# The account that sets the order of instructions: a margin on each TensorE matmul, and a lower DMA rate

## The chip, the cores and the metric

The kernel runs on one NeuronCore of one Trainium2 chip. A core has TensorE (PE, matmuls into PSUM), VectorE (DVE), ScalarE (ACT), GpSimd (POOL) and SyncE (SP, which here issues nearly all DMAs), each with an instruction queue of its own that runs in order. The metric is the device time of one launch in microseconds; several runs are given by their median. Profiles are read by engine and by line of the kernel.

## The reference

It is one inference step of a two-layer trunk over 640 tokens (128 context, 512 latent), width 2048, in fp32:

```python
for l in range(DEPTH):                        # DEPTH = 2, once for context, once for latent tokens
    shift, scale, gate = modulation(c, ada_w[l], ada_b[l])        # silu(c) @ w + b, split in 3
    h = rms_norm(x, norm_g[l]) * (1 + scale) + shift
    if l % 2 == 0:   # [A] windowed attention, 8 heads, sink logit, 2-D rotary  || [B] gated linear attention, 4 heads
        y, _ = even_mixer(h, w_in_even[e], ...)
    else:            # [C] 2-D neighbourhood attention, 8 heads, learned bias    || [D] spatial-gating MLP, 8 column tiles
        y, _ = odd_mixer(h, w_in_odd[o], ...)
    x = x + gate * ((y * silu(gate columns)) @ w_out[l])
y = rms_norm(x, final_norm_g)
```

The projections (`h @ w_in`, `y @ w_out`) make up most of the matmul work. The outputs are the normed tokens, and keys, values and scan states of the context.

## The kernel before

Activations are kept transposed, features on the 128 partitions, tokens along the free axis. A "chunk" is 128 output columns of a weight matrix. Each fp32 product is made of three matmuls on a rounded high part and a low rest: `acth*whi`, `actl*whi`, `acth*wlo`, in halves of 320 (or 322) columns. These "main matmuls" are some 11,900 of the 13,136 PE instructions. Weights come by DMA into `wraw` or `rs`, ACT rounds them into `whi` (in the first stage `suhi`), POOL or DVE subtracts to get `wlo` (`sulo`). Many chunk pairs share work by a Strassen-like scheme with sums of activations (`eh`, `el`, `tail`) and of weights.

No hardware scheduler and no fixed text decides the order. While the program is built, a class `Pace` keeps an account: a clock for each engine (`t["t"]` for PE, `v`, `a`, `g` for DVE, ACT, POOL, `q` for DMA issue, `d` for the DMA stream), and for each piece of a tile when it will be written and read. `Trunk.now` is the account's PE time. After each main matmul or two, `tick` is called: it emits DMAs whose buffer is free by the account, weight splits (`wpump`) whose engines are not too far ahead, deferred evacuations, and one or more steps of generator tasks (a softmax block, a transposition, a scan). A task that needs a result waits with `until`, which lets PE go on with main matmuls as long as the account says that the result is not there yet:

```python
def left(self, *aps):          # how long until these are ready, by the account
    return max(0.0, pc.ready("t", [], spans) - self.now)
def until(self, *aps):
    while not self.force and self.left(*aps) > 0.05:
        yield self.left(*aps)
```

So the account's prices set where the small matmuls and transpositions of the tasks stand among the main matmuls, in which order DVE, ACT, POOL and SP get their instructions, and nothing else: the real waits are semaphores.

The first stage, `start`, is of its own kind. Sixteen times (feature tile f = 0 to 15) four 512 KB pieces of modulation weights (`Y<-ada` and `more<-ada`, a ring of ten buffers) go through four narrow matmuls each (line 1603, 32 output partitions, written `bank<-Y,cond` or `bank<-more,cond`; the trace has two records for each). ACT copies the sums to `adas`, PE turns them (`bank<-ident,adas`, line 401), DVE makes scale and shift from them (`sh`, `A`), ACT and DVE make `acth` and `actl` of tile f, POOL adds the tile's squares (`ssq`). Between these stand the main matmuls of the first eight chunks. Chunks 0 and 1 ("lead", banks 67 to 70) run along with f; chunks 2 to 7 run in "windows" of 2 to 4 tiles into banks 73 and 74, and DVE adds each window to a sum in SBUF (`Y<-Y,bank`, `tail<-tail,bank`, `part_b<-part_b,bank`). A window can start when DVE has emptied its bank.

Every engine instruction but PE's is recorded at line 210, main matmuls at 396, DMA issues at 434.

Of the kernel before, what the change touches and what calls it, by code (L numbers as in the profile page):

```python
# [235 lines left out]
class Trunk:  # L236
# [166 lines left out]
    def pe(self, cost, out, *ins, narrow=False):  # L403
        pc = self.pace
        o, i = [pc.span(out)], [pc.span(x) for x in ins]
        if pc.late:
            pc.due(o + i)
        at = pc.ready("t", o, i)
        if narrow != self.narrow:
            self.narrow = narrow  # L410
            at = max(self.now, at) + 0.15
        self.now = pc.t["t"] = max(self.now, at) + cost
        pc.note("t", o, i, self.now)

    narrow = False
# [6 lines left out]
    def dma(self, out, in_):  # L422

        pc = self.pace
        o, i = [pc.span(out)], [pc.span(in_)]
        if pc.late:
            pc.due(o + i)
        n = int(np.prod(out.shape)) * 4

        def emit():  # L430
            at = pc.t["q"] = max(pc.t["q"], self.now, pc.ready("q", o, i)) + 0.45
            pc.t["d"] = max(pc.t["d"], at + 1.2) + max(0.09, n / 400e3)
            pc.note("q", o, i, pc.t["d"] + 1.0)
            self.nc.sync.dma_start(out, in_)  # L434

        if pc.ready("q", o, i) <= self.now + 0.1:
            emit()
        else:
            pc.late.append((emit, o + i, lambda: pc.ready("q", o, i)))
# [2622 lines left out]
```

## Time and profile before

| | |
|---|---|
| median of 3 runs | 2100.67 us (2098.91 to 2102.41) |
| the profiled execution's own time | 2107.35 us |
| its span, first to last instruction | 2105.6 us |
| mean granted TensorE clock in it | 0.989 of full |
| busy shares of the span: PE, DVE, POOL, ACT | 97%, 72%, 52%, 46% |
| instructions | 38934 |

The profile lists busy time by engine, the span in 40 slices, who waited for whom, and instructions in order of time. Matmuls overlap each other in the records, so the pitch from start to start tells more of PE than the length of one. The profiled execution is 6.7 us above the median of the runs.

### The profile page before, as it was taken

The page shows a single profiled execution, that of the slowest core. Times are in us where ns is not written, and L with a number is a line of the kernel's source. Part 1 is how long each engine was busy: PE and PEld are TensorE (multiplying, and loading weights), DVE is VectorE, ACT ScalarE, POOL GpSimd, SP SyncE. Part 2 cuts the span into 40 slices and gives each one's busy share as a digit, 9 for nine tenths or more (in the row PEclk, how much of TensorE's full clock was granted, in tenths as well). Part 3 has the DMA queues.
Part 4 walks back from the last instruction along what each step waited for, and adds up shares of the span by engine and source line. Part 5 has one row for each costly group of instructions (what it writes and reads, how often), then busy time and mean ns, then how long its engine had stood idle before and what let it go on. Part 6 is the DMA issues. An engine that isn't in the chain of part 4 may idle for free. (4 is left out here: it accounts for less than half of the span.)

```text
span 2105.6 us, 38934 instructions
## 1 busy us (share of the span) xinstructions
PE 2041.9 (97%) x13930; PEld 1969.8 (94%) x13930; DVE 1519.5 (72%) x3468; ACT 964.1 (46%) x2001; POOL 1091.3 (52%) x827
## 2 busy tenths in 40 slices
PE   7899999999999999999999999999999999999996
PEld 4688999999999999999989999999999999999995
DVE  2447788887878787798766878878775567676565
ACT  4334454343334545444454444445554554454443
POOL 3346333233222223566556666756566567757783
PEclk9999999999999999999999999999999999999998
DMA  9943334346544443777648867756655575567766
GB/s 375 377 156 116 124 111 132 123 128 197 167 147 140 122 141 116 245 247 224 177 145 272 269 199 226 244 195 207 229 186 185 180 259 189 197 222 224 237 198 209
DMA packets 215874, 412.52 MB, mean 196 GB/s; under 512 B 25664, under 2 KB 88320, under 8 KB 215680
## 3 DMA queue, kind: packets, MB, share of 16 engines
q1 hardware_dynamic: 214208, 408.43, 58.8%
q8 instruction: 109, 1.79, 0.3%
q10 hardware_dynamic: 1472, 1.61, 0.2%
q14 instruction: 85, 0.70, 0.1%
HBM read 368.88 MB, written 38.45 MB: 193 GB/s over the span
## 5 line engine op out<-in xcount | busy, mean ns | idle before, releaser
L396 PE MATMUL bank<-acth,whi 128*128 128x320 f32 (+1 forms) x3112 | 958.4, 319 | 21.1 <-DVE part_b L210 6.5
L396 PE MATMUL bank<-acth,wlo 128*128 128x320 f32 (+1 forms) x3112 | 932.8, 311 | 3.4 <-POOL wlo L210 3.3
L396 PE MATMUL bank<-actl,whi 128*128 128x320 f32 (+1 forms) x3112 | 931.1, 311 | 0.0
L210 POOL TENSOR_TENSOR wlo<-wraw,whi 128x512 fp32r<-128x512 f32 x359 | 501.7, 1403 | 687.1 <-ACT whi L210 633.5
L396 PEld LDWEIGHTS bank<-acth,whi 128*128 128x128 f32 x3112 | 580.9, 190 | 36.6 <-issue 12.3
L396 PEld LDWEIGHTS bank<-acth,wlo 128*128 128x128 f32 x3112 | 580.2, 189 | 6.4 <-POOL wlo L210 6.0
L396 PEld LDWEIGHTS bank<-actl,whi 128*128 128x128 f32 x3112 | 580.7, 190 | 1.8
L210 POOL TENSOR_TENSOR wlo<-rs,whi 128x512 fp32r<-128x512 f32 x293 | 407.6, 1404 | 205.6 <-ACT whi L210 172.9
L210 ACT ACTIVATE whi<-wraw 128x512 fp32r<-128x512 f32 x393 | 241.2, 624 | 178.4 <-PE bank L396 101.1
L210 ACT ACTIVATE whi<-rs 128x512 fp32r<-128x512 f32 x329 | 198.9, 624 | 82.9 <-PE bank L396 52.1
L210 DVE CUSTOM_DVE_ANT_0 adas<-adas,bank,partg 128x256 bf16<-128x256 f32 (+1 forms) x320 | 178.0, 556 | 22.3 <-ACT bank L210 11.8
L396 PE MATMUL bank<-tail,whi 128*128 128x322 f32 (+1 forms) x672 | 152.2, 314 | 0.2 <-DMA tail<-far_dram 0.2
L210 ACT ACTIVATE arena<-arena,bc 128x128 f32<-128x128 f32 (+3 forms) x167 | 83.4, 519 | 137.7 <-DVE bc L210 97.0
L396 PE MATMUL bank<-eh,whi 128*128 128x322 f32 (+1 forms) x444 | 138.9, 313 | 0.0
L396 PE MATMUL bank<-eh,wlo 128*128 128x322 f32 (+1 forms) x444 | 137.8, 310 | 0.5 <-DVE wlo L210 0.5
L396 PE MATMUL bank<-el,whi 128*128 128x322 f32 (+1 forms) x444 | 137.9, 311 | 0.0
L210 ACT ACTIVATE Y<-bank 128x128 f32<-128x128 f32 (+5 forms) x134 | 52.0, 410 | 143.3 <-PE bank L396 73.0
L210 ACT ACTIVATE sums<-bank 128x320 f32<-128x320 f32 (+1 forms) x125 | 54.4, 435 | 129.7 <-PE bank L396 122.3
L210 DVE TENSOR_TENSOR rs<-rs 128x512 f32<-128x512 f32 x83 | 92.9, 1129 | 28.5 <-POOL wlo L210 23.4
L396 PEld LDWEIGHTS bank<-tail,whi 128*128 128x128 f32 x672 | 112.2, 189 | 0.8 <-DMA tail<-far_dram 0.8
L210 DVE TENSOR_TENSOR bank<-bank,sums 128x320 f32<-128x320 f32 (+1 forms) x162 | 76.3, 492 | 50.1 <-PE bank L396 41.3
L396 PE MATMUL bank<-tail,wlo 128*128 128x322 f32 (+1 forms) x336 | 104.0, 310 | 0.4 <-POOL wlo L210 0.4
(227 smaller groups left out, 2886.6 us busy)
## 6 DMA issues: line engine op xcount, KB each, us to landing
tail<-far_dram SPq DMA_DIRECT2D x196, 322.0 KB, 4.5
wraw<-w_even SPq DMA_DIRECT2D x176, 256.0 KB, 3.3
adas<-ada_g SPq DMA_DIRECT2D x128, 256.0 KB, 3.8
adas<-ada SPq DMA_DIRECT2D x128, 256.0 KB, 3.6
rs<-w_odd SPq DMA_DIRECT2D x63, 512.0 KB, 5.4
wraw<-w_odd SPq DMA_DIRECT2D x37, 512.0 KB, 5.4
more<-ada SPq DMA_DIRECT2D x36, 512.0 KB, 8.1
rs<-w_out SPq DMA_DIRECT2D x30, 512.0 KB, 5.5
```

Of the source, the lines that this page charges most:

```text
L210: return f(*args, **kw)
L396: self.nc.tensor.matmul(out, lhsT, rhs, start=start, stop=stop, **kw)
```

## The change

Two prices of the account are changed, and nothing else:

```diff
@@ def pe(self, cost, out, *ins, narrow=False): @@
-        self.now = pc.t["t"] = max(self.now, at) + cost
+        self.now = pc.t["t"] = max(self.now, at) + cost + 0.0025
@@ def dma(self, out, in_): emit() @@
-            pc.t["d"] = max(pc.t["d"], at + 1.2) + max(0.09, n / 400e3)
+            pc.t["d"] = max(pc.t["d"], at + 1.2) + max(0.09, n / 330e3)
```

The price of a 320-column main matmul goes from 0.1473 to 0.1498 us, that of a 512 KB transfer from 1.31 to 1.59 us. PE has the same 13,136 instructions, SP the same 1388 DMAs. Three weight subtractions go from DVE (364 to 361 of that shape) to POOL (661 to 664), and ACT has 24 table loads in place of 30. The main matmuls after the first stage stand in the same order as before; what stands between them moves.

First place, PE in the first stage, at the tiles f = 4 and 5: `bank_72<-ident,adas` are the transpositions after which DVE can make the next tile's `actl`. Before:

```order
L401 MATMUL bank_72<-ident,adas 128x128 x2
L396 MATMUL bank_74<-acth,whi 128x320
L396 MATMUL bank_74<-actl,whi 128x320
L396 MATMUL bank_74<-acth,wlo 128x320
L396 MATMUL bank_74<-acth,whi 128x320
L396 MATMUL bank_74<-actl,whi 128x320
L396 MATMUL bank_74<-acth,wlo 128x320
L1603 MATMUL bank_71<-more_116,cond_112 32x256 x8
L396 MATMUL bank_73<-acth,suhi_225 128x322
```

Now:

```order
L401 MATMUL bank_72<-ident,adas 128x128 x2
L396 MATMUL bank_73<-acth,whi 128x322
L396 MATMUL bank_73<-actl,whi 128x322
L396 MATMUL bank_73<-acth,wlo 128x322
L396 MATMUL bank_73<-acth,whi 128x322
L396 MATMUL bank_73<-actl,whi 128x322
L396 MATMUL bank_73<-acth,wlo 128x322
L1603 MATMUL bank_71<-more_116,cond_112 32x256 x4
L396 MATMUL bank_74<-acth,whi 128x320
```

The transpositions stand one group of six earlier among the window matmuls (after the 108th main matmul of the program, before after the 114th), and the narrow matmuls come piece by piece (x4) where two pieces (x8) stood together. In the whole stage the 64 pieces make 47 separate groups, where they made 33, and the last piece comes after the 480th main matmul, where it came after the 384th.

Second place, DVE in the first stage, around main matmul 228 (tile f = 9 before, f = 8 now): `actl` belongs to the next tile, `tail` and `part_b` empty the window banks. Before:

```order
L210 TENSOR_TENSOR tail_81<-tail_81,bank_74 128x320
L210 SCALAR_TENSOR_TENSOR actl<-Y,A_98,acth 128x128
L210 SCALAR_TENSOR_TENSOR actl<-Y,A_98,acth 128x512
L210 TENSOR_TENSOR actl<-sh_771,acth 128x2
L210 TENSOR_TENSOR tail_81<-tail_81,bank_73 128x320
L210 TENSOR_TENSOR part_b<-part_b,bank_73 128x2
```

Now:

```order
L210 TENSOR_TENSOR part_b<-part_b,bank_73 128x2
L210 SCALAR_TENSOR_TENSOR actl<-Y,A_98,acth 128x128
L210 SCALAR_TENSOR_TENSOR actl<-Y,A_98,acth 128x512
L210 TENSOR_TENSOR actl<-sh_742,acth 128x2
L210 TENSOR_TENSOR tail_81<-tail_81,bank_74 128x320
L210 TENSOR_TENSOR tail_81<-tail_81,bank_73 128x320
L210 TENSOR_TENSOR part_b<-part_b,bank_73 128x2
```

The three `actl` instructions stand one bank earlier: ahead of the addition of bank 74 that they followed.

Third place, PE in an even layer's attention head: `bank_71<-ident,arena` turns the context block's softmax, after DVE has scaled it. Before:

```order
L396 MATMUL bank_69<-acth,whi 128x320
L396 MATMUL bank_69<-actl,whi 128x320
L396 MATMUL bank_69<-acth,wlo 128x320
L401 MATMUL bank_71<-ident,arena_4477 128x128
L396 MATMUL bank_67<-acth,whi 128x322
L396 MATMUL bank_67<-actl,whi 128x322
```

Now:

```order
L396 MATMUL bank_69<-acth,wlo 128x320
L401 MATMUL bank_71<-ident,arena_4474 128x128
L396 MATMUL bank_72<-Y,arena_4474 128x128
L396 MATMUL bank_72<-arena_4474 128x128
L396 MATMUL bank_72<-Y,arena_4474 128x256
L396 MATMUL bank_69<-acth,whi 128x320
L396 MATMUL bank_69<-actl,whi 128x320
```

The transposition stands nine main matmuls earlier (after the 3063rd, before after the 3072nd), and the next block's score matmuls (`bank_72<-Y,arena`) come right behind it.

## The prediction

> **What bounds the kernel now.** I read the page first: the busy line of PE, and the slices.
>
> ```profile
> PE 2041.9 (97%) x13930; PEld 1969.8 (94%) x13930; DVE 1519.5 (72%) x3468; ACT 964.1 (46%) x2001; POOL 1091.3 (52%) x827
> ...
> PE   7899999999999999999999999999999999999996
> ...
> PEclk9999999999999999999999999999999999999998
> DMA  9943334346544443777648867756655575567766
> GB/s 375 377 156 116 124 111 132 123 128 197 167 147 140 122 141 116 245 247 224 177 145 272 269 199 226 244 195 207 229 186 185 180 259 189 197 222 224 237 198 209
> ```
>
> PE is the bound in nearly every slice, and the change gives it the same matmuls. What can change is the time in which PE has none: 2105.6 - 2041.9 = 63.7 us idle, and what a lowered clock costs. DMA is full only in the first two slices. Next, the pitch of the stream, from the instructions in order of time:
>
> ```profile
> 1000.00 0.31 PE L396 MATMUL bank<-actl,whi 128*128 128x320 f32 x1
> ...
> 1007.97 0.31 PE L396 MATMUL bank<-el,whi 128*128 128x320 f32 x1
> ```
>
> There are 54 steps between these two starts: 7.97 / 54 = 0.1476 us. The account charged 0.1473, which was right to 0.2%; with the margin it charges 0.1498, 1.5% more than the chip takes. So the margin doesn't mend a wrong price; what it does must come from the moved order.
>
> Then the waits of PE, longest first, with their total, number and longest:
>
> ```profile
> PE bank L1603 <- DMA Y<-ada: 7.4, 4, 6.7
> PE bank L396 <- DVE part_b L210: 6.5, 3, 3.5
> PE bank L396 <- DVE tail L210: 5.9, 2, 4.3
> ...
> PE bank L401 <- DVE arena L210: 3.6, 4, 1.3
> ...
> PE bank L396 <- DVE sums L210: 2.7, 1, 2.7
> PE bank L401 <- ACT Y L210: 1.9, 1, 1.9
> ...
> PE bank L396 <- DVE r L210: 1.7, 1, 1.7
> ```
>
> They are few and each has a place. The first 6.7 is the first DMA's landing and stays. Stretches show what follows a long wait (us from the start, busy time of PE, PEld, DVE, ACT, POOL, then granted clock, DMA share, GB/s):
>
> ```profile
> 0.00:100.00 100.00, 82.63 (x662) 56.25 (x666) 35.76 (x86) 37.70 (x90) 36.38 (x33) 0.91 0.99 379
> ...
> 56.00:60.00 4.00, 0.81 (x6) 0.54 (x4) 4.00 (x4) 1.84 (x3) 4.00 (x4) 0.96 1.03 403
> 60.00:66.00 6.00, 5.65 (x29) 4.05 (x30) 1.25 (x5) 0.13 (x1) 1.04 (x1) 0.50 1.03 402
> ...
> 94.00:97.00 3.00, 3.00 (x16) 1.85 (x16) 0.56 (x2) 0.38 (x1) 0.00 (x0) 0.50 0.91 355
> ...
> 1148.00:1152.00 4.00, 4.00 (x21) 3.96 (x20) 3.63 (x9) 1.72 (x4) 3.32 (x3) 0.57 0.84 264
> ...
> 200.00:210.00 10.00, 8.34 (x55) 7.88 (x54) 6.84 (x16) 6.50 (x10) 1.79 (x2) 1.00 0.38 127
> ```
>
> After the wait that ends at 60 the clock is at half for 6 us and more, after the second one on `part_b` (it ends at 92) for some 3, after the one on `Y` at 1147 for most of 4. The wait of 1.7 on `r` lies in 200:210, where the clock stays at 1.00. So here a wait of about 1.9 us and more is paid a second time: half of 3 to 7 us.
>
> **The change part by part, first stage.** The two prices act together, and I take them by place. (a) Narrow matmuls come in more groups. Their cost from the timeline:
>
> ```profile
> 33.60 1.07 PE L1603 MATMUL bank<-Y,cond 128*32 128x256 f32 x16
> 34.49 0.61 PE L1603 MATMUL bank<-more,cond 128*32 128x256 f32 x8
> 35.03 0.41 PE L396 MATMUL bank<-acth,whi 128*128 128x320 f32 x1
> ...
> 36.10 0.64 PE L1603 MATMUL bank<-more,cond 128*32 128x256 f32 x8
> 36.67 0.56 PE L396 MATMUL bank<-acth,suhi 128*128 128x322 f32 x2
> ```
>
> Three pieces in one group take 35.03 - 33.60 = 1.43, one alone 0.57; three alone would take 1.71, so a group costs 0.14 beside its pieces. 47 groups for 33: 14 x 0.14 = +2.0 us. Nothing hides it, since PE is the path.
>
> (b) The two long waits on `part_b`. DVE and POOL at the first of them:
>
> ```profile
> 53.01 0.17 DVE L210 TENSOR_REDUCE sh<-bank 128x4 f32<-128x16 f32 x1 [5.38 <-PE bank L401]
> ...
> 55.28 3.15 DVE L210 SCALAR_TENSOR_TENSOR actl<-Y,A,acth 128x128 fp32r<-128x128 f32 x2 [1.63 <-ACT acth L210]
> 58.35 1.48 DVE L210 TENSOR_TENSOR actl<-sh,acth 128x2 fp32r<-128x2 f32 x1
> ...
> 55.03 1.58 POOL L210 TENSOR_TENSOR ssq<-ssq,adas 128x640 f32<-128x640 f32 x1 [3.73 <-ACT adas L210]
> 56.56 1.31 POOL L210 TENSOR_TENSOR sulo<-wraw,suhi 128x512 fp32r<-128x512 f32 x1
> 57.84 1.98 POOL L210 TENSOR_TENSOR ssq<-ssq,adas 128x640 f32<-128x640 f32 x1
> ...
> 68.62 0.35 DVE L210 SCALAR_TENSOR_TENSOR actl<-Y,A,acth 128x128 fp32r<-128x128 f32 x1 [0.34 <-ACT acth L210]
> 69.23 0.75 DVE L210 SCALAR_TENSOR_TENSOR actl<-Y,A,acth 128x512 fp32r<-128x512 f32 x1 [0.26 <-ACT acth L210]
> 69.90 0.15 DVE L210 TENSOR_TENSOR actl<-sh,acth 128x2 fp32r<-128x2 f32 x1
> ...
> 60.35 0.64 PE L396 MATMUL bank<-acth,whi 128*128 128x322 f32 x1 [3.54 <-DVE part_b L210]
> ```
>
> With POOL idle (68 to 70) the three `actl` take 1.25 us; with three POOL instructions in a row beside them (55 to 60) 4.6, and the additions that empty the window banks stand behind. So from the transpositions to the empty bank it is 60.35 - 53.01 = 7.3 us in the bad case, and 3.3 less, 4, without POOL's. What PE has to do in between, before: 18 main matmuls and a group of two pieces, 18 x 0.1476 + 1.00 = 3.66. Now, from the order, 24 main matmuls and three pieces in two groups: 24 x 0.1476 + 0.57 + 1.00 = 5.1. At the second place `actl` stands one bank earlier, with 18 main matmuls and three pieces alone, 4.4 us, between the transpositions and the first bank needed. Of the later tiles one has less room (f = 6: 12 main matmuls and two pieces alone, 2.9), the others 4 to 12. Bad case everywhere: the waits stay; good case everywhere: they go. The bad case needs POOL's work in three in a row, which two of 16 tiles had, so I take the good one: -5.5 of the 6.5 us (the third wait, 1 us, stays). With them go the halves of the clock, about 6.8 us at 60 and 3.4 at 94: -3.4 and -1.7.
>
> On the clock, a page of the Trainium skill speaks against this term: "TensorE: Matmul & The Clock Gate", Part 1, says that TensorE falls back to half after at least one idle window of about 3.4 us. By that only the first wait (3.54) lowers the clock and only 3.4 us go, and the sum below would end 1.7 higher. The trace has half the clock at 94 after a shorter wait, so I keep 5.1.
>
> (c) New short waits: at f = 6 (2.9 us of cover for a chain of 3.1 to 4) and at f = 2 (six main matmuls fewer behind the transpositions). 0 to 4 us, I take +2.0. First stage: +2.0 - 5.5 - 5.1 + 2.0 = -6.6, between +4 (waits stay, groups and new waits come) and -8.6.
>
> **After it.** (d) The margin lets each matmul count for more, so a task that waits for DVE or ACT comes back after fewer of them; the chip's engines are no faster for it. The third place shows it: in the trace its transposition waited.
>
> ```profile
> 622.12 0.31 PE L396 MATMUL bank<-acth,wlo 128*128 128x320 f32 x1
> 623.44 0.33 PE L401 MATMUL bank<-ident,arena 128*128 128x128 f32 x1 [1.01 <-DVE arena L210]
> ```
>
> Nine matmuls earlier and with DVE's row of instructions the same, it waits 9 x 0.1476 = 1.3 us more. Other blocks go the other way by as much. The heads' waits (`DVE arena` at L401) are 3.6 now: bounds -3.6 and, if each of 16 heads had half of this place's loss, +10; I take +2.5, nearer to none, since shifts of both signs stand in the order. The gated linear attention ahead has three such places with 1 or 2 us less: +1.0 (0 to +3).
>
> (e) The wait on `ACT Y` at 1147 and its clock, 1.9 + 1.7: the transposition stands 108 matmuls later with the same 12 matmuls of cover, beside other ACT work. -3.6 or 0: -1.8.
>
> (f) The long waits on `tail` (4.3, at 1067) and `sums` (2.7, at 1915) and the last 120 matmuls: the rows of all engines around them are the same, 0. The three subtractions moved to POOL (1.4 us each, POOL 52% busy) and six table loads fewer on ACT (46% busy) lie beside PE, 0; if ACT gains 6 x 1.28 us where PE waits, that is below (d)'s lower bound. The DMA price itself: pieces landed 1.24 to 1.28 us apart, 512 KB each, some 410 to 420 GB/s:
>
> ```profile
> 8.12 1.08 PE L1603 MATMUL bank<-Y,cond 128*32 128x256 f32 x8 [0.38 <-DMA Y<-ada]
> 9.36 1.08 PE L1603 MATMUL bank<-Y,cond 128*32 128x256 f32 x8 [0.17 <-DMA Y<-ada]
> 10.64 1.08 PE L1603 MATMUL bank<-Y,cond 128*32 128x256 f32 x8 [0.20 <-DMA Y<-ada]
> ```
>
> So 400 was near the chip and 330 is low: pieces will lie in the ring longer, and no wait of PE on DMA comes of it: 0.
>
> Sum: -6.6 + 2.5 + 1.0 - 1.8 = -4.9 against the profiled 2107.35, 2102.5; against the median of the runs, 2100.67 - 4.9 = **2095.8 us**.
>
> **Rivals.** Slower: term (d) at its upper end. The place is the transpositions behind each softmax block, 16 heads of 5 blocks. One main matmul (0.148) too early at each is 80 x 0.148 = 11.8 us. For it: the account was exact on PE, and DVE's 1.24 us instructions beside POOL are dearer than in its price. Against: only four such waits in the trace. It decides from 7 us on; at 11.8 in place of 2.5 the time is 2105.1. Second, the first stage's gain is taken back at f = 6: if POOL has three in a row there, the chain is 7.3 against 2.9, a wait of 4.4 and 3.4 of clock, +7.8 for the 2.0 of (c): 2101.6, no change. Third, the order moves and the sum of waits is as before in all places: 2100.67 + 2.0 for the groups, 2102.7.
>
> **How the numbers follow.** A measurement of this kernel can tell about 0.2%, 4.2 us, from no change. Likeliest: 0.45, its own range 2088 to 2100, with 0.09 of it above 2096.5. Slower rival 0.23; the second 0.17; the third 0.15, of which a little ends beyond 4.2. Faster: 0.36 of the likeliest and 0.08 from the lower ends of the others, 0.44; same 0.31; slower 0.25. The range to hold 8 of 10 goes from the likeliest's lower end less the heads' waits, 2086, to beyond the slower rival, 2108.
>
> **What would show it.** In the profile after: no wait on `part_b` over 2 us, and the clock at full from 30 to 1060, show (b); 47 groups of narrow matmuls, (a). Waits of PE L401 on `DVE arena` near 6 us instead of 3.6 show (d). `tail` 4.3 and `sums` 2.7 again show (f). A wait over 3 us around 75 with half the clock behind it would make the prediction wrong, as would a sum of L401 waits above 10.

## Result and the profile after

The changed kernel took 2085.36 us (median of 5 runs, 2084.72 to 2089.41), the one before 2100.67 (5 runs, 2096.24 to 2102.63). The ratio is 0.9933, 95% interval 0.9917 to 0.9949: 11 to 17 us faster, where 4.9 were forecast. The direction was right; the size was a third of it, and the time lies 0.6 us below the range given. The profiled execution took 2084.72 us, span 2082.9, so the two profiles differ by 22.6 us. Some 7 of that is the old kernel's profiled execution, slower than all of its unprofiled runs.

The page of the changed kernel, busy line and slices as shown of before:

```profile
PE 2036.0 (98%) x13930; PEld 1963.8 (94%) x13930; DVE 1503.7 (72%) x3465; ACT 959.6 (46%) x1995; POOL 1097.9 (53%) x830
...
PEclk9999999999999999999999999999999999999998
DMA  9954333345554434776648856756665575567756
GB/s 374 359 173 134 124 119 124 122 137 184 159 169 142 128 127 132 232 253 221 205 132 274 269 192 231 253 198 213 219 197 192 179 258 190 191 222 244 249 186 217
```

PE's idle time is 2082.9 - 2036.0 = 46.9 us, 16.8 less. Its waits, by what ended them (total, number, longest, us):

```profile
PE bank L1603 <- DMA Y<-ada: 7.4, 4, 6.5
...
PE bank L401 <- DVE arena L210: 3.3, 2, 1.8
...
PE bank L396 <- DVE tail L210: 2.4, 2, 1.9
...
PE bank L396 <- DVE r L210: 1.7, 1, 1.7
...
PE bank L396 <- DVE part_b L210: 0.7, 1, 0.7
...
PE bank L401 <- ACT Y L210: 0.4, 1, 0.4
```

`part_b` went from 6.5 to 0.7 as forecast. But `tail` fell too (its wait of 4.3 at 1067 became two of 1.9 and 0.5), `Y` from 1.9 to 0.4, and `sums` with its 2.7 is gone: three waits far behind the first stage, two of which the prediction put at no change. The half clock (stretches of the changed kernel; us, then the busy time of PE, PEld, DVE, ACT and POOL, and the granted clock third from the end):

```profile
22.00:30.00 8.00, 6.09 (x29) 4.50 (x26) 1.59 (x5) 3.29 (x7) 5.54 (x5) 0.57 1.03 408
60.00:66.00 6.00, 5.35 (x42) 3.99 (x42) 3.15 (x9) 0.40 (x2) 2.65 (x2) 1.00 1.03 402
94.00:97.00 3.00, 3.00 (x27) 2.72 (x29) 1.56 (x5) 1.96 (x5) 2.12 (x2) 1.00 0.93 289
200.00:204.00 4.00, 4.00 (x19) 4.00 (x18) 2.95 (x7) 3.79 (x6) 0.28 (x2) 0.57 0.47 166
1060.00:1064.00 4.00, 3.73 (x16) 3.33 (x14) 1.32 (x3) 2.11 (x4) 1.34 (x2) 0.57 0.67 246
1146.00:1150.00 4.00, 4.00 (x30) 3.99 (x29) 3.57 (x12) 1.24 (x4) 2.70 (x2) 1.00 0.46 143
```

It is full at 60, 94 and 1146 now. At 22 it is at half for 6.8 us, as in the profile of before, and it is new at half at 200, behind the wait on `r` that had left it at 1.00 before.

What the prediction hadn't read is who else waits for DMA. ACT, before:

```profile
ACT whi L210 <- DMA wraw<-w_odd: 16.5, 6, 6.0
```

and in the changed kernel:

```profile
ACT whi L210 <- DMA wraw<-w_odd: 3.6, 1, 3.6
```

### The profile page after: what moved, and what is told of

Same layout as the page of the kernel before. It is cut to its first block, busy times and chain, and to the rows that moved or that the text cites. A ratio compares the mean times of both kernels' runs of the same rounds, so it can differ in the third digit from the quotient of the medians.

```text
span 2082.9 us, 38915 instructions
## 1 busy us (share of the span) xinstructions
PE 2036.0 (98%) x13930; PEld 1963.8 (94%) x13930; DVE 1503.7 (72%) x3465; ACT 959.6 (46%) x1995; POOL 1097.9 (53%) x830
## 5 line engine op out<-in xcount | busy, mean ns | idle before, releaser
L210 DVE TENSOR_TENSOR rs<-rs 128x512 f32<-128x512 f32 x83 | 85.5, 1036 | 31.8 <-POOL wlo L210 31.4
```

The source lines that it names most:

```text
L210: return f(*args, **kw)
```

## Experiments

Theories: A, the prediction's split (first stage gains, later a small loss, the DMA price does nothing); B, the DMA price gains after the first stage, since ACT and DVE no longer have instructions in their queues whose data isn't there; C, the margin gains there; D, any shift reshuffles the waits, and the result is luck.

### The two prices and the two parts of the program apart

Both prices became attributes, and a line at the end of the first stage can give them other values (the lines that differ from the kernel before):

```diff
-        self.now = pc.t["t"] = max(self.now, at) + cost
+        self.now = pc.t["t"] = max(self.now, at) + cost + self.margin
...
-    narrow = False
+    narrow = False; margin, rate = 0.0025, 330000.0
...
-            pc.t["d"] = max(pc.t["d"], at + 1.2) + max(0.09, n / 400e3)
+            pc.t["d"] = max(pc.t["d"], at + 1.2) + max(0.09, n / self.rate)
...
-        self.actset, self.soon = "s", 99.0
+        self.actset, self.soon = "s", 99.0; self.margin, self.rate = 0.0, 400000.0
```

This is the kernel with both prices in the first stage alone. The others have other values in these lines; where the prices hold everywhere, the last line is that of before.

Margin alone:

> Only the margin of 2.5 ns on each matmul; DMA priced as before. In the built program the narrow matmuls keep their 33 groups and the first stage is nearly that of before, so the first stage's gain isn't here. Theory A (the prediction's split): the gain lies in the first stage, the margin brings transpositions too early later on: 2101 to 2104. Theory B (rate): the gain after 1000 us comes from the DMA price, since ACT's waits for w_odd went from 16.5 to 3.6 us: 2099 to 2102, those waits again near 16. Theory C (margin): the waits of PE after 1000 us (tail, Y, sums, some 11 us with their clock) go by the margin: 2087 to 2092.

DMA price alone:

> Only the DMA price (330 for 400); no margin. The program has 50 groups of narrow matmuls and the last piece where the changed kernel has it. Theory A: the first stage's gain, 2094 to 2098, and nothing later. Theory B: first stage and later waits both gain: 2084 to 2089, ACT's waits for w_odd under 6 us. Theory C: first stage alone, 3.6 us as between the two traces: 2096 to 2098.

Both, in the first stage alone:

> Both prices changed, but only until the end of the first stage (some 185 us); then the old ones. Theory A: 2092 to 2096. Theories B and C: the 3.6 us that the two traces show by the 1000th main matmul, 2096 to 2098, and the waits on tail, Y and sums later as before. If any change of place upstream reshuffles the later waits by chance (theory D), it lies anywhere between 2085 and 2100.

Both, after the first stage alone:

> The old prices in the first stage, both new ones from its end on. Theory A: 2101 to 2104. Theories B and C: the gain after the first stage, 2087 to 2091, with the part_b waits (6.5 us) as before and tail, Y, sums short. Theory D: as for the kernel before this one, 2085 to 2102.

DMA price after the first stage:

> Old prices in the first stage; from its end on only the DMA price is new (330). Theory B (the rate keeps ACT's splits out of the queue until their weights are there): waits on Y near matmul 6200 and on sums at 10782 gone, as in the run with the rate alone, the part after the first stage 8 us shorter: 2088 to 2092. Theory C (the margin): the waits stay, 2096 to 2100. Theory D (any move reshuffles the waits): anywhere from 2086 to 2100, with other waits instead.

Margin after the first stage:

> Old prices in the first stage; from its end on only the margin is new. The run with the margin alone has tail at 2.0 and no wait on sums, but 4.3 on Y with the clock at half for 6.8 us behind it: by B 2093 to 2097, with the Y wait; by C 2087 to 2091.

The changed kernel again:

> The changed kernel once more, beside the other three on one chip: by its first comparison 0.9933 of the time of the kernel before, 2082 to 2087 if that stands near 2098; its waits as in its first trace, but clock halves after waits of 2 to 3 us may come or stay away.

Ratios to the kernel before, with 95% intervals. It stood at 2097.9 us in both series; the changed kernel's 0.9933 is the comparison above, against 2100.67:

| | first stage only | after it only | everywhere |
|---|---|---|---|
| margin | not run | 0.9998 [0.9985, 1.0011] | 0.9976 [0.9965, 0.9988] |
| DMA price | not run | 0.9967 [0.9955, 0.9979] | 1.0007 [0.9997, 1.0017] |
| both | 1.0002 [0.9992, 1.0013] | 0.9958 [0.9943, 0.9973] | 0.9933 [0.9917, 0.9949]; again 0.9945 [0.9932, 0.9958] |

Medians in us: margin 2092.97, DMA price 2099.59, both in the first stage 2098.63, both after it 2088.86, DMA price after it 2089.16, margin after it 2095.44, the changed kernel again 2085.13.

The expected times were met where the stages were parted: both after the first stage (B and C), the DMA price after it (B), the margin after it (B), the changed kernel again. The first three were not: the margin alone lies 1 us above the range of C and 6 under that of B, the DMA price alone above all three ranges, both in the first stage 0.6 us above the range of B and C and inside D's wide one.

So the gain lies after the first stage, and there it is the DMA price's: -6.9 us (0.0033 x 2098), against -0.4 for the margin and -8.8 for both. In the first stage the two nearly cancel: by division the DMA price costs 1.0007 / 0.9967, +8.4 us, and the margin brings 0.9976 / 0.9998, -4.6; measured together they make +0.4, where these two add up to +3.8. The traces agree with a large effect of each: the 1000th main matmul starts at 241.6 us with the DMA price alone and at 226.4 with the margin alone, against 229.4 to 232.2 in three kernels with the old first stage (next table). A and C are wrong. First-stage and later effect add up to -8.4; the changed kernel has -11.5 to -14. The intervals cover the smaller of these differences and nearly the larger; what it is stays open, and with it how much of D (a shift reshuffles the waits) is in it.

The place of the later gain, from the traces (start of the n-th main matmul, counted in order; us between):

| kernel | to 1000 | 1000 to 5000 | 5000 to 6500 | 6500 to the end |
|---|---|---|---|---|
| before | 234.2 | 724.4 | 239.9 | 907.1 |
| margin everywhere | 226.4 | 723.8 | 242.5 | 898.1 |
| DMA price everywhere | 241.6 | 722.0 | 235.1 | 900.4 |
| both, first stage | 231.4 | 723.5 | 240.9 | 901.2 |
| margin after it | 229.4 | 723.9 | 240.7 | 899.0 |
| DMA price after it | 232.2 | 720.9 | 234.6 | 898.3 |
| both after it | 229.8 | 724.2 | 232.7 | 897.0 |
| changed kernel | 230.6 | 722.1 | 232.7 | 897.5 |

Among these, 5000 to 6500 falls from 240 to 243 us to 233 to 235 wherever the later DMA price is 330, and only there. PE's waits within it, added up, are 7.2 to 9.7 us in the four kernels with the old later price and 3.3 to 5.6 in the four with the new one. The profile of before is the slow one also in the last column. PE's waits in the first-stage kernel, over the whole span:

```profile
PE bank L396 <- DVE tail L210: 4.1, 1, 4.1
...
PE bank L396 <- DVE sums L210: 3.2, 2, 2.2
PE bank L401 <- ACT Y L210: 2.7, 1, 2.7
```

with the margin after the first stage:

```profile
PE bank L401 <- ACT Y L210: 4.2, 2, 3.8
PE bank L396 <- DVE tail L210: 4.0, 3, 1.9
```

and with the DMA price after it, where no `sums` is left and `Y` is short:

```profile
PE bank L396 <- DVE tail L210: 4.5, 3, 1.9
...
PE bank L401 <- ACT Y L210: 1.0, 2, 0.6
```

`tail` doesn't tell the two prices apart. Its wait after the 5709th main matmul, 4.3 us before and 4.1 here, is 1.9 with the margin after the first stage and 1.0 with the DMA price after it (with another of 1.9 eighteen matmuls on). `Y` does: the margin makes it longer, the DMA price shorter.

How a late transfer reaches PE stands in the kernel with the margin alone, one row each of DVE, ACT and PE, in order of time:

```profile
1149.73 0.48 DVE L210 CUSTOM_DVE_ANT_0 adas<-adas,bank,partg 128x256 bf16<-128x256 f32 x1 [5.70 <-DMA adas<-ada_g]
...
1155.36 0.81 ACT L210 ACTIVATE bank<-adas 128x256 f32<-128x256 f32 x2 [6.51 <-DVE partg L210]
...
1157.68 0.47 PE L401 MATMUL bank<-ident,Y 128*128 128x128 f32 x1 [4.09 <-ACT Y L210]
```

DVE stands 5.70 us before a reduction whose data hasn't landed. ACT needs the row of reductions that follows and stands 6.51 for it; `Y` comes after in ACT's queue, and PE waits 4.09 for `Y`. The waits of ACT and DVE that a DMA ended, all rows added up, come to 128 to 151 us in the kernels with the old later DMA price (before 76.4 + 74.8; first stage 128.2; margin 148.0; margin later 143.3) and to 82 to 102 with 330 (DMA price 81.8; later 94.8; both later 102.3; the changed kernel 95.9, again 93.0). They fall as B says. That a wait of PE comes from them is shown at this place; the sums alone don't show it for the others.

### One transfer of small pieces

Why did `tail` wait 4.3 us before, and 1.9 in the changed kernel? ACT, before:

```profile
1051.58 0.42 ACT L210 ACTIVATE eh<-bank 128x320 fp32r<-128x320 f32 x1
1058.01 0.63 ACT L210 ACTIVATE whi<-wraw 128x512 fp32r<-128x512 f32 x1 [6.01 <-DMA wraw<-w_odd]
1058.55 0.73 ACT L210 ACTIVATE acth<-Y 128x640 fp32r<-128x640 f32 x1
```

It stands for a weight piece, and `acth`, on which DVE and PE depend, is queued behind. The DMAs issued from 1043 to 1053 (KB each, us from issue to landing):

```profile
wraw<-w_odd SPq DMA_DIRECT2D x4, 256.0 KB, 7.4
arena<-xT SPq DMA_DIRECT2D x2, 320.0 KB, 3.8
...
far_dram<-fs SPq DMA_DIRECT2D x1, 24.0 KB, 8.8
```

24 KB in 3072 pieces of 8 bytes took 8.8 us, and the four weight pieces came behind it. The account charges it 0.09. SP issued it after the 5598th main matmul. In the changed kernel SP issues it after the 5583rd, and ACT's wait behind it is the 3.6 us shown above; the margin alone moves it about as far (5586th, `tail` 1.8). So this part of the gain is not the DMA price's alone. The experiment moves the transfer alone to ACT's DMA queue:

```diff
-            self.dma(e.bitcast(U32), self.fs.bitcast(U32))
+            nc.scalar.dma_start(e.bitcast(U32), self.fs.bitcast(U32))
```

> The kernel before, with one DMA moved from SP to ACT's queue: far_dram<-fs, 24 KB in 8-byte pieces, which landed 5.4 us after the one ahead of it and held up four weight pieces behind it, for which ACT waited 6.0 us and, behind ACT and DVE, PE 4.3 us on tail. Theory E (that one transfer makes the tail wait): tail under 1.5 us and no half clock near 1067: 2091 to 2095. Rival (the small pieces keep the same 16 engines busy from any queue): tail 3 to 4.5 as before, 2097 to 2099.

It took 2094.96 us against 2099.43: 0.9976 [0.9964, 0.9988]. PE, DVE and POOL have the same instructions in the same order as before. ACT at the same place:

```profile
1051.58 0.63 ACT L210 ACTIVATE whi<-wraw 128x512 fp32r<-128x512 f32 x1 [1.76 <-DMA wraw<-w_odd]
```

1.76 for 6.01, and the wait of 4.3 on `tail` is gone. But the edit changed the time as well as the queue: ACT issues the transfer after the 5560th main matmul, 38 earlier than SP did. What the DMA engines did from 1041 to 1051, in slices of 0.25 us, and one of the DMAs issued then:

```profile
DMA  9999999654202020797979669985979999998999
GB/s 349 322 194 158 78 49 25 8 5 4 1 0 1 0 10 0 61 82 92 113 51 113 92 143 266 266 236 225 352 317 399 375 379 387 328 322 311 363 385 402
...
tail<-x1T_dram SPq DMA_DIRECT2D x1, 320.0 KB, 5.4
```

The small pieces went from 1041.1 to 1044.5, at first with the engines full and the rate falling, and the four weight pieces were issued from 1045.0 on: they did not run side by side, the small ones were through before. Nor does the other queue part them from the rest. The load in the last line, which SP issued at 1043.6 with nothing ahead of it on its own queue, took 5.4 us to land; the same load before, issued ahead of the small pieces, took 3.0. That is what the rival said, and its time was wrong because it left out the earlier issue. All 14 profiles fit: the wait on `tail` after the 5709th main matmul is 4.3 and 4.1 us where the transfer was issued after the 5598th and the 5601st, 1.0 to 2.7 where after the 5578th to the 5588th, and none where after the 5560th. That the other queue brought anything by itself isn't shown.

E holds for that wait, not for the whole place, and its other two signs failed: 18 matmuls later a `tail` wait of 1.9 us appears that wasn't there before, and the clock is at half for 3.4 us behind it (6.8 before). The time is at the upper end of its range.

The Trainium skill, "DMA: Bandwidth & Descriptors", Specifications, names 512 B as the least size of a transfer at line rate; the trace agrees, with 24 KB in 8.8 us.

### Mixes and sizes

The margin everywhere with the DMA price at 330 after the first stage and 400 in it:

> Margin everywhere; the DMA price 330 only from the end of the first stage on, 400 in it. If the stages add up (the margin alone reached main matmul 1000 at 226.4 us, the changed kernel at 230.6, and the changed kernel takes some 1854 from there): 2080 to 2083, under the changed kernel. If the later waits depend by chance on what came before (D): 2084 to 2093.

2083.56 us, 0.9938 [0.9926, 0.9951], beside 0.9945 for the changed kernel in the same series: within the intervals the same, and between the two expected ranges, so it decides nothing about D. Its trace reached main matmul 1000 at 229.1 us, not 226.4: the first stage had a second half clock at 23 us in this execution.

The same with the small transfer on ACT's queue:

> The same move in the kernel with the margin everywhere and the DMA price 330 after the first stage (tail waits 1.7 and 2.1, half a clock of 3.4 us behind them). E: both waits under 1 us, 2079 to 2082. Rival: 2083 to 2085.

2083.01 us, 0.9924 [0.9908, 0.9941]. The first `tail` wait went, the second stayed, at 1.8 us for 1.9. The time lies at the near end of the rival's range, and the step to the mix is smaller than the intervals: inconclusive.

A DMA price of 270 after the first stage:

> As the mix, with a DMA price of 270 in place of 330 after the first stage. If the waits of ACT and DVE for DMA cost the time and fall further (under 85 together): 2078 to 2082. If 330 is past most of them, others come (weights split too late, PE waiting for whi or wlo): 2085 to 2092.

2109.24 us, 1.0051 [1.0033, 1.0069]: slower than before, and above both ranges. The waits of ACT and DVE for DMA didn't fall (105.2 us together, 99.8 in the mix), and PE itself waits for loads of activations now, not for `whi` or `wlo` as expected:

```profile
PE bank L396 <- DMA tail<-far_dram: 11.5, 5, 4.3
...
PE bank L396 <- DMA acth<-t_dram: 5.7, 2, 3.6
```

The DMA slices from 1144 to 1158, where three of the waits on `tail<-far_dram` lie, are empty just ahead of them:

```profile
DMA  0000066000195999999978999799999989678899
```

The real DMA was nearly idle for some 4 us while loads that PE needs next had not been issued. SP's own waits show what held them: from 1138.4 to 1145.0 it stood 6.7 us for POOL's `tail`, whose store `far_dram<-tail` is ahead of those loads in its queue and was through at 1146.8; POOL had itself stood 3.6 us for ACT's `whi`. In the mix SP issues the same store 54 main matmuls earlier (after the 6267th, here the 6321st). Why the lower rate places it so late was not tested. Of the three rates tried with the margin, 330 is the best: 2092.97 us at 400, 2083.56 at 330, 2109.24 at 270.

The old prices with every landing 0.5 us later after the first stage:

```diff
-    narrow = False
+    narrow = False; land = 1.0
...
-            pc.note("q", o, i, pc.t["d"] + 1.0)
+            pc.note("q", o, i, pc.t["d"] + self.land)
...
-        self.actset, self.soon = "s", 99.0
+        self.actset, self.soon = "s", 99.0; self.land = 1.5
```

> Prices of the kernel before, but after the first stage the account has every transfer land 0.5 us later (1.5 behind its stream's end in place of 1.0), at the old rate and without margin. Theory B1 (what counts is that ACT and DVE aren't given work before its data is there): their waits for DMA fall from some 130 to 150 us together to 110 or less, and the time to 2088 to 2093, as with the rate. Theory B2 (what counts is the rate, in backlogs): waits stay above 120, 2095 to 2100.

2081.78 us (2081.37 to 2082.45), 0.9917 [0.9900, 0.9935], with neither of the two new prices: the lowest median of all, 3.4 to 3.6 us under the changed kernel's in its two series, each with its own runs of before; the intervals of the ratios overlap. So a new rate isn't needed for the gain, against B2. But B1 isn't confirmed either: the time lies 6 us under its range, and the waits of ACT and DVE for DMA are 57.5 + 56.3 = 113.8, not 110 or less. A part of the gain lies elsewhere: 1000 to 5000 takes 717.8 us for 724, where PE's L401 waits on the heads' `arena` are gone; 5000 to 6500 takes 234.5. Why the heads gain isn't shown.

```profile
PE bank L396 <- DVE part_b L210: 6.5, 3, 3.5
PE bank L396 <- DVE tail L210: 4.1, 2, 2.1
```

These are its longest waits but the first DMA's: `part_b` as before, `Y` and `sums` not among them.

## Why the prediction was right and wrong

**(a) Groups, +2.0.** The 47 groups came; they cost more. The price took the pieces and left out the neighbours. A lone piece in the changed kernel:

```profile
31.53 0.31 PE L396 MATMUL bank<-actl,suhi 128*128 128x322 f32 x1
31.68 0.31 PE L396 MATMUL bank<-acth,sulo 128*128 128x322 f32 x1
31.92 0.64 PE L1603 MATMUL bank<-Y,cond 128*32 128x256 f32 x8
32.49 0.41 PE L396 MATMUL bank<-acth,suhi 128*128 128x320 f32 x1
32.74 0.31 PE L396 MATMUL bank<-actl,suhi 128*128 128x320 f32 x1
```

The matmul ahead takes 0.24 to the next start and the one behind 0.25, in place of 0.148: 0.19 more for each group. Estimated from this one place, 14 x (0.14 + 0.19) = +4.6. The groups are the DMA price's (50 with it alone, 33 with the margin alone), not of both together.

**(b) `part_b`, -5.5, and its clock, -5.1.** The waits went, by 5.8. The clock term was one execution's draw. Five other kernels have the first stage of before instruction for instruction; the kernel with both prices only after it shows, with the same waits of 3.5 and 2.0 us,

```profile
60.00:66.00 6.00, 6.00 (x64) 4.09 (x62) 1.89 (x7) 1.38 (x4) 0.00 (x0) 0.85 1.03 401
...
94.00:97.00 3.00, 3.00 (x41) 1.94 (x40) 2.16 (x7) 2.00 (x5) 0.23 (x1) 1.00 1.03 399
```

Over the six, the first wait cost 3.4 us at half clock in five and 6.8 in one; the second nothing in four and 3.4 in two. Half of that is lost: on average (5 x 3.4 + 6.8) / 6 / 2 + (2 x 3.4) / 6 / 2 = 2.6 us, not 5.1; and 1.7 us came back at 200, behind `r`, so the clock was not full from 30 to 1060 as forecast. Of the Trainium skill's rule that the prediction weighed ("TensorE: Matmul & The Clock Gate", Part 1: half after at least one idle window of some 3.4 us) this case keeps a part: the wait of 3.5 always lowered the clock, the shorter one in two of six.

**(c) New waits, +2.0.** On PE `suhi`, `more` and `adas` together wait 2.6 us more in the first stage, and the 1.5 on `sulo` is gone: +1.1, right in sign, though nothing came at f = 6.

**First stage, -6.6.** Measured +0.4 [-1.7, +2.7]. In the trace of before the 744th main matmul starts at 187.0 us, in the five others at 182.1 to 185.1, in the changed kernel at 183.8: the baseline was the slow end of a scatter. This is the step that failed on the gain's side: a sum made against one execution whose clock had fallen badly, with the groups at less than half of what they cost. It also left out two spells of half clock. One at 22 us, 3.4 us lost, is in all three profiles with the new first stage and in two of the six with the old; the one at 200, 1.7 us lost, in three of three and in one of six. An estimate from these averages, groups +4.6, waits -5.8, their clock -2.6, new waits +1.1, the spell at 22 +2.3, the one at 200 +1.4, comes to +1.0, inside the measured interval. Whether the new order brings these spells, three profiles can't show.

**(d), +3.5 with the gated attention ahead.** The wait at the third place grew, but by 0.45 us from start to start (1.32 to 1.77), not by 1.3; others went: `DVE arena` at L401 is 3.3 for 3.6, not 6, and 1000 to 5000 changed by -2.3 us in the profiles. The sign of the sum was wrong, by 5.8 us.

**(e) `Y`, -1.8.** Gone but for 0.4, with its clock: -3.2. The DMA price did it; the margin alone made `Y` longer.

**(f) `tail` and `sums` 0, DMA price 0.** This is the mechanism that was missed, and it is most of what lies between the forecast and the result: the later DMA price alone is worth 6.9 us. "No wait of PE on DMA comes of it" was nearly true (0.9 us more on `more<-ada`); the price works through ACT and DVE. That the rows around `tail` are the same was true of PE and POOL; on ACT two `whi` and on DVE one `actl` stand elsewhere in the 150 main matmuls ahead of it. It was no ground for an equal wait in any case, because the small transfer was issued 15 main matmuls earlier and landed earlier. With their clock `tail` and `sums` gave (4.3 - 2.4) + 2.7 and half of 3.4 + 3.4 us, 8.0 between the two profiles. Not all of that is the DMA price's: with the margin alone after the first stage that `tail` wait is 1.9 too and `sums` is gone, but `Y` took back what they gave.

The slower rivals: the heads' waits did not come, and at f = 6 no wait over 1.0 us came. The third, waits moved about and no gain, fits the first stage alone. That the forecast had the right direction is luck: the gain that it counted on did not come, and the gain that came it had put at nothing. By mechanism only (a)'s count, (b)'s waits and the signs of (c) and (e) were right.

## What to carry to other kernels

Where an account or a hand-written order places work, read who waits for DMA on every engine, not only on the one that is the bound: an instruction on ACT or DVE whose data lands 5 us late holds back all that is queued behind it, and the bound engine's wait then names another tile. A price on the late side (here 0.5 us on each landing) was worth 17 us, while a rate much further on the same side (270 for 400, with the margin) had PE wait for its loads and lost 10. Look also at where a transfer of small pieces is issued: issuing one of them 38 matmuls earlier, from another queue, took a wait of 4.3 us off PE. Before a term is sized by the clock or by a wait in one trace, look at the scatter of runs: the profiled one of before was 7 us above its median, more than the gain that was forecast.

## What had not been expected of the hardware

One DMA of 24 KB in 8-byte pieces took 8.8 us from issue to landing and held up four weight pieces of 256 KB behind it. Issued from ACT's queue it still slowed what SP issued: a load of 320 KB took 5.4 us to land in place of 3.0. The half clock comes in spells of 3.4 us or twice that (once, in the kernel with 270, three times that; only the spell at the end of the program is longer). The same order with the same wait draws more or fewer of them from execution to execution: the wait of 3.5 us on `part_b` one or two, the wait of 2.0 none or one. After the wait of 1.7 us on `r` the clock stayed full in the profile of before and fell to half at 200 us in the changed kernel's.
